# Gated delta net: decay times, their operands and a mask product moved from GpSimd to VectorE

## The chip, the cores and the metric

One core of one Trainium2 chip runs the whole program in one launch. The metric is device time in microseconds (us), the median of the runs of one kernel. A profile is one further execution, recorded instruction by instruction. The engines are named as in its rows: PE (TensorE matmul) and PEld (its weight loads), DVE (VectorE), ACT (ScalarE), POOL (GpSimd), SP (SyncE, which issues the DMAs).

## The reference

A decoder layer for 2048 tokens of width 1024: an RMS norm, one input projection, four head groups side by side (retention, gated delta net, S5, gated linear attention), a gate for each, and one output projection. The change touches the gated delta net: 4 heads of width 64, in chunks of 64 tokens.

```python
gcum = jnp.cumsum(gc, axis=-1)
decay = jnp.exp(jnp.where(tri, gcum[..., :, None] - gcum[..., None, :], -jnp.inf))
kb = kc * bc[..., None]
a_mat = jnp.where(strict, jnp.einsum('bhnid,bhnjd->bhnij', kb, kc) * decay, 0.0)
sol = lax.linalg.triangular_solve(jnp.eye(c, dtype=F32) + a_mat, rhs, left_side=True, lower=True)
attn = jnp.einsum('bhnid,bhnjd->bhnij', qc, kc) * decay
def step(state, inp):
    v_new = u_n - jnp.einsum('bhcd,bhde->bhce', w_n, state)
    o = jnp.einsum('bhcd,bhde->bhce', qg_n, state) + jnp.einsum('bhij,bhje->bhie', attn_n, v_new)
    state = state * gl_n[..., None, None] + jnp.einsum('bhcd,bhce->bhde', kg_n, v_new)
```

## The kernel before, in words

Tokens lie in 16 tiles of 128 (two chunks each). The delta net (`phase_dn`) goes over 8 pairs of tiles, called u = 0 to 7, in rounds that overlap: round s runs the convolution and the decays of pair s (`conv` with `dn_pre` inside), the scores and the inverse of pair s-1 (`dn_front`, `dn_sub`) and the recurrence of pair s-2 (`dn_back`). A round lasts some 45 us, and the whole stretch runs from about 600 to 975 us of the span.

What the steps of the prediction name:
- `dgx`: operands of the decays, g (fp16) spread over 64 columns times a mask, 128x512 for each tile. TensorE multiplies them by constant matrices (L1568), ScalarE takes the exponential into `dE` (L1569).
- `dmb`: decay times mask (strict and not strict side by side), 128x512 for each tile, and then times `dD` (beta over the key's squared norm). `dD` comes at the end of a string of small VectorE operations (`dkk`, `dry`, `drt`).
- `dLT` and `dST` (L1638 and L1643 in the code, shown as L153 in rows because a helper records them): scores from PSUM (ring `t`, L1627) times `dmb`. `dLT` is written to memory and read back transposed for the inverse: a string of 28 small VectorE operations on `dsV` and `dgm`. The transposes L1660 need the slot in ring `t` that the last `dST` frees.
- `VS`, L1813: the state's subtraction on VectorE, four in a round (two tiles, two chunks). TensorE waits for it at L1818.
- `cva`: the convolution's multiply-adds, 128x256; `ckq` and `cv` close them. `raw` (L1473, ScalarE) takes the convolution's input out of PSUM, `pa` (L309, L301) are the projections that fill TensorE between the steps.
- `fss`, `fry`, `frt`, `frr`, `fsq`: the norm and gating of a finished tile (`finish`).

The order on each engine is set when the program is built: a scheduler places instructions by priority and by its own estimates, buffers of a pool are reused in turn, and each engine then runs its list strictly in order. `dgx` has two buffers, so that a `dgx` may start when the L1568 of two `dgx` before has read its buffer, long before its own L1568 needs it.

Of the kernel before, what the change touches and what calls it, by code (L numbers as in the profile page):

```python
# [11 lines left out]
ALU = mybir.AluOpType  # L12
# [143 lines left out]
class Trunk:  # L156
# [1388 lines left out]
    def dn_pre(self, u, kq, out):  # L1545

        nc, NT = self.nc, self.NT
        P = self.dP  # L1550
        mask2 = self.c("mask2")
        tl = slice(2 * u, 2 * u + 2)
        gms = []
        for t in range(2):
            gm = self.t(P, [128, 256], "dgx", bufs=2).bitcast(F16).rearrange("p (g t) -> p g t", t=64)
            gms.append(gm)
            nc.gpsimd.tensor_tensor(gm, self.g16[:, 2 * u + t].rearrange("p a h -> p (a h)").unsqueeze(2).to_broadcast([128, 8, 64]), mask2[:, 64:128].unsqueeze(1).to_broadcast([128, 8, 64]), op=ALU.mult)
        yield
        E = self.t(P, [128, 2, 2, 4, 64], "dE", bufs=1)
        mb = self.t(P, [128, 2, 4, 2, 64], "dmb", bufs=1)  # L1560
        for t in range(2):
            gmf = gms[t].rearrange("p (a h) t -> p a (h t)", a=2)
            if t == 1:
                yield
            pe = self.ps("t")
            for j in range(2):
                for a in range(2):
                    nc.tensor.matmul(pe[:, j * 256:j * 256 + 256], self.sums16[:, j], gmf[:, a], start=(j == 0 and a == 0), stop=(j == 1 and a == 1))  # L1568
            nc.scalar.activation(E[:, t].rearrange("p a h t -> p (a h t)"), pe, AF.Exp)  # L1569
            nc.gpsimd.tensor_tensor(mb[:, t], E[:, t, 0].unsqueeze(2).to_broadcast([128, 4, 2, 64]),  # L1570
                                    mask2.rearrange("p (s t) -> p s t", s=2).unsqueeze(1).to_broadcast([128, 4, 2, 64]), op=ALU.mult)
        yield
        kq = kq[u]
        sq = self.t(P, [128, 2, 2, 256], "dsq", bufs=1)
        nc.scalar.activation(sq.rearrange("p s j t -> p (s j t)"), kq.rearrange("p s j t -> p (s j t)"), AF.Square)
        yield
        ps = self.ps("t")[:, 0:16]
        for t in range(2):
            for s in range(2):
                for j in range(2):  # L1580
                    o = t * 8 + s * 4 + j * 2
                    nc.tensor.matmul(ps[:, o:o + 2], sq[:, s, j, t * 128:t * 128 + 128], self.c("halves"), start=True, stop=True)  # L1582
        at = self.count["t"]

        ops = []
        V = Later(nc.vector, ops)
        p4 = ps.rearrange("p (t s h) -> p t s h", t=2, s=2)
        epsq = self.t(P, [128, 2, 4], "depsq", bufs=3)
        V.tensor_scalar(epsq, p4[:, :, 1], 4 * EPS, 16384 * EPS, op0=ALU.add, op1=ALU.mult)
        kk = self.t(P, [128, 8], "dkk")  # L1590
        k24 = kk.rearrange("p (t h) -> p t h", t=2)
        V.tensor_scalar(k24, p4[:, :, 0], 4 * EPS, None, op0=ALU.add)
        rk, more = self.rsqrt_ops(P, kk, None, 8, "dr")
        ops.extend(more)
        sk = self.t(P, [128, 8], "dsk")
        V.tensor_tensor(sk, kk, rk, op=ALU.mult)
        V.tensor_tensor(rk, rk, rk, op=ALU.mult)
        r24 = rk.rearrange("p (t h) -> p t h", t=2)
        D = self.t(P, [128, 2, 4], "dD")
        V.tensor_tensor(D, self.beta[:, tl, :], r24, op=ALU.mult)  # L1600
        kgd = self.t(P, [128, 2, 4], "dkgd", bufs=3)
        V.tensor_tensor(kgd, self.kgd[:, tl, :], r24, op=ALU.mult)
        gl = self.t(P, [128, 2, 4], "dgl", bufs=3)
        nc.gpsimd.tensor_copy(gl, E[:, :, 1, :, 63])
        for t in range(2):
            V.tensor_tensor(mb[:, t].rearrange("p h s i -> p h (s i)"), mb[:, t].rearrange("p h s i -> p h (s i)"),
                            D[:, t].unsqueeze(2).to_broadcast([128, 4, 128]), op=ALU.mult)
        out.update(gl=gl, epsq=epsq, kgd=kgd, sk=sk, E=E, mb=mb)
        self.string(18, 2, ops, "t", at)
        yield  # L1610
# [371 lines left out]
```

## Time and profile before

| what | value |
|---|---|
| median of 3 runs | 1224.54 us (1223.58 to 1227.66) |
| the profiled execution's own time | 1231.87 us |
| its span, first to last instruction | 1229.8 us |
| mean granted TensorE clock, as a share of full speed | 0.959 |
| PE busy in the span | 1116.9 us |
| DVE busy in the span | 911.0 us |
| POOL busy in the span | 471.1 us |

The profiled execution is 7.3 us over the median of the runs shown, and 2.1 us of its time lie outside the span. Times of instructions are read from the span, so differences worked out there are taken off the median.

### The profile page before, as it was taken

What the parts mean: (1) busy time and instruction counts of PE and PEld (TensorE: products, weight loads), DVE (VectorE), ACT (ScalarE), POOL (GpSimd) and SP (SyncE); (2) the same over time, 40 slices, a digit from 0 to 9 for tenths busy, and PEclk for the clock granted to TensorE, in tenths of its full rate; (3) what the DMA queues carried; (4) which work ended last, traced back from release to release, by engine and by line L of the source; (5) the groups of instructions that cost most, each with busy time, mean ns of one, the idle gap of its engine ahead of it and who ended that gap; (6) DMA issues with size and microseconds to landing.
All of it is one profiled execution on the core that took longest, in us unless ns stands there. A gap on an engine that the chain in (4) does not pass through costs nothing. (4 is left out here: it accounts for less than half of the span.)

```text
span 1229.8 us, 38305 instructions
## 1 busy us (share of the span) xinstructions
PE 1116.9 (91%) x15687; PEld 929.8 (76%) x15687; DVE 911.0 (74%) x3237; ACT 505.7 (41%) x1124; POOL 471.1 (38%) x848
## 2 busy tenths in 40 slices
PE   3889999999999999989779889898899999899996
PEld 2767788888878887877667677677777877788885
DVE  6779655445888788887797877877787744778885
ACT  5733322124444444453454344344443533443431
POOL 3112111111676666563552432533522312444433
PEclk9899999999989999999998998999899989999999
DMA  8565611201121111221212121211123616567652
GB/s 288 146 168 129 173 62 35 70 31 57 26 61 36 36 35 36 65 61 23 88 46 34 28 42 18 61 27 34 30 58 81 181 44 194 140 187 177 183 138 86
DMA packets 186911, 104.97 MB, mean 85 GB/s; under 512 B 158000, under 2 KB 173552, under 8 KB 184560
## 3 DMA queue, kind: packets, MB, share of 16 engines
q1 hardware_dynamic: 186160, 102.00, 32.1%
q8 instruction: 123, 2.02, 0.7%
q10 hardware_dynamic: 576, 0.52, 0.1%
q14 instruction: 52, 0.43, 0.1%
HBM read 59.43 MB, written 26.23 MB: 70 GB/s over the span
## 5 line engine op out<-in xcount | busy, mean ns | idle before, releaser
L301 PEld LDWEIGHTS <-xT 128*128 128x128 f16 x3456 | 337.4, 101 | 78.3 <-issue 22.0
L301 PE MATMUL pa<-w,xT 128*128 128x256 f16 x3072 | 384.4, 280 | 7.4 <-DVE w L265 3.3
L309 PE MATMUL pa<-xT,w 128*128 128x256 f16 x1536 | 202.4, 281 | 8.8 <-ACT raw L1473 7.0
L309 PEld LDWEIGHTS <-w 128*128 128x128 f16 x1536 | 147.7, 101 | 35.6 <-issue 11.1
L1858 PE MATMUL o<-w,yT 128*128 128x256 f16 x1344 | 155.5, 276 | 7.4 <-DMA yT<-y 7.3
L1858 PEld LDWEIGHTS <-yT 128*128 128x128 f16 x1344 | 132.5, 99 | 27.9 <-DMA yT<-y 10.0
L153 DVE SCALAR_TENSOR_TENSOR cva<-raw,cw,cva 128x256 f32<-128x256 f32 x144 | 80.3, 559 | 22.3 <-ACT cva L1478 20.8
L1869 POOL TENSOR_TENSOR ot<-of,npost 128x256 f32<-128x256 f32 x64 | 56.3, 898 | 50.7 <-ACT of L1867 50.7
L153 ACT ACTIVATE gE<-gE 128x384 f32<-128x384 f32 x96 | 45.6, 516 | 56.2 <-DVE gE L153 26.4
L153 DVE TENSOR_REDUCE fss<-fsq 128x4 f32<-128x256 f32 x48 | 19.8, 413 | 56.6 <-ACT fsq L408 56.6
L1472 POOL COPY raw<-raw 128x3 f32<-128x3 f32 x48 | 19.5, 413 | 110.1 <-DVE cva L153 75.1
L301 PE MATMUL pa<-wsu,xT 128*128 128x280 f16 x384 | 52.9, 298 | 7.4 <-DMA xT<-h 3.6
L265 DVE SCALAR_TENSOR_TENSOR w<-stg,wgs,w 128x256 f16<-128x256 f32 x96 | 50.3, 580 | 9.6 <-POOL w L262 9.6
L1147 POOL TENSOR_TENSOR ropq<-ropm,ropn 128x256 f32<-128x256 f32 x16 | 12.8, 797 | 113.4 <-DVE ropn L1144 105.4
L408 ACT ACTIVATE fsq<-o 128x256 f32<-128x256 f32 x48 | 18.2, 379 | 82.1 <-PE o L1195 57.5
L1868 DVE SCALAR_TENSOR_TENSOR ojk<-of 128x256 f32<-128x256 f32 x64 | 40.0, 625 | 14.2 <-ACT of L1867 11.7
L371 ACT ACTIVATE th<-pa,hd 128x256 f32<-128x256 f32 x64 | 30.1, 470 | 42.8 <-PE pa L301 40.4
L1484 ACT ACTIVATE cvt<-cva 128x256 f32<-128x256 f32 x48 | 20.0, 416 | 65.0 <-DVE cva L153 64.8
L1179 POOL TENSOR_TENSOR sg<-sbd,cst 64x128 f32<-64x128 f32 x30 | 12.8, 425 | 80.4 <-DVE sbd L1180 68.8
L1299 PE MATMUL sc<-gE 32*32 32x32 f32 (+1 forms) x2944 | 39.7, 200 | 1.5 <-DVE KK L910 1.5
L1299 PEld LDWEIGHTS sc<-gE 32*32 32x32 f32 (+1 forms) x2944 | 33.8, 105 | 8.8 <-issue 2.1
L1804 POOL TENSOR_TENSOR dKG<-dkh,dkgd 64x256 f32<-64x256 f32 x32 | 21.9, 683 | 47.2 <-PE c L1818 47.2
(420 smaller groups left out, 2329.1 us busy)
## 6 DMA issues: line engine op xcount, KB each, us to landing
x<-in_x SPq DMA_DIRECT2D x16, 512.0 KB, 4.4
stg<-in_wi SPq DMA_DIRECT2D x8, 1024.0 KB, 5.0
yo<-y_d SPq DMA_DIRECT2D x14, 512.0 KB, 4.4
xo<-in_x SPq DMA_DIRECT2D x14, 512.0 KB, 3.6
out<-xo SPq DMA_DIRECT2D x13, 512.0 KB, 3.8
y_d<-fsq SPq DMA_DIRECT2D x48, 128.0 KB, 1.8
xT<-in_wi SPq DMA_DIRECT2D x4, 1024.0 KB, 7.5
rope<-in_rope SPq DMA_DIRECT2D x16, 256.0 KB, 3.0
```

Of the source, the lines that this page charges most:

```text
L153: return lambda *a, **k: self.ops.append(lambda: getattr(self.engine, name)(*a, **k))
L265: nc.vector.scalar_tensor_tensor(dst[:, 1, k, :], st[:, k, :], gs[:, k:k + 1], dst[:, 0, k, :], op0=ALU.mult, op1=ALU.subtract)
L301: yield lambda k=k, i=i, a=a, b=b: self.nc.tensor.matmul(out, xt[:, a, k, t0:t0 + 128], w[:, b, k, :], start=(k == 0 and i == 0), stop=(k ...
L309: yield lambda k=k, i=i, a=a, b=b: self.nc.tensor.matmul(out, w[:, b, k, c0:c0 + 128], xt[:, a, k, :], start=(k == 0 and i == 0), stop=(k ...
L371: nc.scalar.activation(th, ps[0], AF.Tanh, scale=self.half(dsc))
L1299: nc.tensor.matmul(box[0][po:po + pn, e, c0:c0 + rh.shape[1]], lh[r], rh[r], start=True, stop=True, tile_position=(32 * (2 * hp + e), col))
L1472: nc.gpsimd.tensor_copy(x[:, 0:3], x[:, 256:259])
L1484: nc.scalar.activation(th[0], a, AF.Tanh, scale=0.5)
L1804: nc.gpsimd.tensor_tensor(KG[r, c], f["kh"][r, t], f["kgd"][r, t, :].unsqueeze(2).to_broadcast([64, 4, 64]), op=ALU.mult)
L1858: nc.tensor.matmul(o, yT[:, a, k, :], w[:, b, k, :], start=(k == 0 and q == 0 and j % per == 0), stop=(k == 7 and q == 2 and j % per == pe ...
L1868: nc.vector.scalar_tensor_tensor(jk, of[:, cs], 1.0, of[:, cs], op0=ALU.mult, op1=ALU.mult, accum_out=so[:, j:j + 1])
L1869: nc.gpsimd.tensor_tensor(t1[:, cs], of[:, cs], npost[:, cs], op=ALU.mult)
```

## The change

The two `dgx` of each pair are made on VectorE in place of GpSimd, with the same operands (L1557). GpSimd no longer multiplies decay by mask (L1570). VectorE makes decay times `dD` times mask in one `scalar_tensor_tensor` for each tile and head (128x128 each, eight for a pair), with `dD` as the scalar of each partition, in place of one `tensor_tensor` of 128x512 for each tile.

```diff
-            nc.gpsimd.tensor_tensor(gm, self.g16[:, 2 * u + t].rearrange("p a h -> p (a h)").unsqueeze(2).to_broadcast([128, 8, 64]), mask2[:, 64:128].unsqueeze(1).to_broadcast([128, 8, 64]), op=ALU.mult)
+            nc.vector.tensor_tensor(gm, self.g16[:, 2 * u + t].rearrange("p a h -> p (a h)").unsqueeze(2).to_broadcast([128, 8, 64]), mask2[:, 64:128].unsqueeze(1).to_broadcast([128, 8, 64]), op=ALU.mult)
...
-            nc.gpsimd.tensor_tensor(mb[:, t], E[:, t, 0].unsqueeze(2).to_broadcast([128, 4, 2, 64]),
-                                    mask2.rearrange("p (s t) -> p s t", s=2).unsqueeze(1).to_broadcast([128, 4, 2, 64]), op=ALU.mult)
...
+        m3 = mask2.rearrange("p (s t) -> p s t", s=2)
         for t in range(2):
-            V.tensor_tensor(mb[:, t].rearrange("p h s i -> p h (s i)"), mb[:, t].rearrange("p h s i -> p h (s i)"),
-                            D[:, t].unsqueeze(2).to_broadcast([128, 4, 128]), op=ALU.mult)
+            for h in range(4):
+                V.scalar_tensor_tensor(mb[:, t, h], E[:, t, 0, h].unsqueeze(1).to_broadcast([128, 2, 64]), D[:, t, h:h + 1], m3, op0=ALU.mult, op1=ALU.mult)
```

The scheduler also orders the stretch anew, on all engines but SP. Three places follow. The first is VectorE's list in the round of pair 6's convolution, around the third of the four `VS` of pair 4 (the second tile's first chunk). Before:

```order
L153 COPY dsV_14122<-dsV_14122 64x256
L153 TENSOR_TENSOR frt_14449<-fry_14448 128x4
L153 SCALAR_TENSOR_TENSOR frt_14449<-frt_14449,fss_14446 128x4
L153 SCALAR_TENSOR_TENSOR fry_14448<-frt_14449,fry_14448 128x4
L153 TENSOR_TENSOR frt_14449<-fry_14448 128x4
L153 SCALAR_TENSOR_TENSOR frt_14449<-frt_14449,fss_14446 128x4
L153 SCALAR_TENSOR_TENSOR frt_14449<-frt_14449 128x4
L153 SCALAR_TENSOR_TENSOR fry_14448<-frt_14449,fry_14448 128x4
L1813 TENSOR_TENSOR VS_14246<-dQ_14237,c_14437 64x256
L153 TENSOR_SCALAR frr_14447<-fry_14448,hd_1657_11455 128x4
```

In the changed kernel, at the same place:

```order
L153 TENSOR_TENSOR dgm_14150<-dsV_14146 64x15
L153 SCALAR_TENSOR_TENSOR fry_14471<-frt_14472,fry_14471 128x4
L153 TENSOR_TENSOR dsV_14146<-dsV_14146,dgm_14150 64x15
L153 TENSOR_TENSOR frt_14472<-fry_14471 128x4
L153 COPY dsV_14146<-dsV_14146 64x256
L153 SCALAR_TENSOR_TENSOR frt_14472<-frt_14472,fss_14469 128x4
L1812 TENSOR_TENSOR VS_14270<-dQ_14261,c_14460 64x256
L153 SCALAR_TENSOR_TENSOR frt_14472<-frt_14472 128x4
L153 SCALAR_TENSOR_TENSOR fry_14471<-frt_14472,fry_14471 128x4
L153 TENSOR_SCALAR frr_14470<-fry_14471,hd_1657_11462 128x4
```

The third `VS` stood behind all of the norm's string but its last scale (`frr`); now two more operations of that string come behind it. In the rounds of the convolutions of pairs 3, 4, 5 and 7 the third `VS` has moved ahead of four, four, eight and four small operations.

The second place is VectorE's list from `dD` to `dLT` of pair 6, where the next round begins. Before:

```order
L153 TENSOR_TENSOR dD_14590<-beta_3619,dry_14587 128x8
L153 TENSOR_TENSOR dkgd_14591<-kgd_4207,dry_14587 128x8
L153 SCALAR_TENSOR_TENSOR fsq_14818<-o_14537,frr_14602,dgg_14498 128x64
L153 TENSOR_TENSOR dmb_14398<-dmb_14398,dD_14590 128x512 x2
L153 SCALAR_TENSOR_TENSOR fsq_14818<-o_14537,frr_14602,dgg_14498 128x64 x3
L153 TENSOR_TENSOR dLT_14842<-t_14716,dmb_14398 128x4x64
L153 TENSOR_TENSOR dLT_14842<-t_14717,dmb_14398 128x4x64
```

In the changed kernel:

```order
L153 TENSOR_TENSOR dD_14612<-beta_3619,dry_14609 128x8
L153 TENSOR_TENSOR dkgd_14613<-kgd_4207,dry_14609 128x8
L153 SCALAR_TENSOR_TENSOR fsq_14846<-o_14559,frr_14624,dgg_14520 128x64
L153 SCALAR_TENSOR_TENSOR dmb_14422<-dE_14421,dD_14612,cst_75 128x128 x8
L153 SCALAR_TENSOR_TENSOR fsq_14846<-o_14559,frr_14624,dgg_14520 128x64 x2
L153 TENSOR_TENSOR dLT_14870<-t_14744,dmb_14422 128x4x64
L153 TENSOR_TENSOR dLT_14870<-t_14745,dmb_14422 128x4x64
```

The two `dmb` of 512 columns have become eight of 128 columns, at the same place: behind `dD`, ahead of `dLT`.

The third place is where the `dgx` of pair 7 are made, in the round of pair 6's convolution. Before, on GpSimd:

```order
L1805 TENSOR_TENSOR dKG_14411<-cst_75,dgl_13101 64x256
L1472 COPY raw_1507_10267<-raw_1507_10267 128x3
L1557 TENSOR_TENSOR dgx_15049<-g_709_4199,cst_75 128x512
L1570 TENSOR_TENSOR dmb_14398<-dE_14397,cst_75 128x512
L1688 MEMSET dsV_14879 64x256
L1690 MEMSET dsV_14879 64x16
L1557 TENSOR_TENSOR dgx_15051<-g_709_4199,cst_75 128x512
L1570 TENSOR_TENSOR dmb_14398<-dE_14397,cst_75 128x512
```

In the changed kernel it stands in VectorE's list, between the strings of the inverse and behind the second `VS`:

```order
L1488 SCALAR_TENSOR_TENSOR ckq_14135<-cvt_14353,cva_14310 128x256
L153 TENSOR_TENSOR dgm_14150<-dsV_14146 64x63
L1812 TENSOR_TENSOR VS_13701<-dQ_14261,c_14361 64x256
L153 TENSOR_TENSOR dsV_14146<-dsV_14146,dgm_14150 64x9x7
L1557 TENSOR_TENSOR dgx_15077<-g_709_4199,cst_75 128x512
L153 TENSOR_TENSOR dgm_14150<-dsV_14146 64x60
```

This first `dgx` of a pair waits there for TensorE (its buffer's last reader, L1568); the second stands behind the fourth `VS` and carries no wait. In the first round the two `dgx` of pair 0 stand directly behind the last two `w` (L265) of VectorE's list.

## Rows read from the trace of the kernel before

**Rows 1.** The page: span, and busy time of each engine.
```profile
span 1229.8 us, 38305 instructions
...
PE 1116.9 (91%) x15687; PEld 929.8 (76%) x15687; DVE 911.0 (74%) x3237; ACT 505.7 (41%) x1124; POOL 471.1 (38%) x848
```

**Rows 2.** Windows, delta net: stretch; PE, PEld, DVE, ACT, POOL busy; PEclk, DMA.
```profile
600.00:960.00 360.00, 318.71 (x4905) 255.11 (x4903) 291.35 (x957) 156.60 (x355) 143.97 (x232) 0.94 0.22 49
```

**Rows 3.** Groups on PE, 600 to 975 us: count, busy, mean ns, idle before, releasers.
```profile
L309 PE MATMUL pa<-xT,w 128*128 128x256 f16 x1096 | 146.4, 283 | 7.2 <-ACT raw L1473 7.0
L1818 PE MATMUL c<-VS,dKG 128*64 128x64 f32 x224 | 19.8, 234 | 15.0 <-DVE VS L1813 6.3 <-DVE frr L153 5.0 <-DVE fry L153 2.1
L1582 PE MATMUL t<-cst,dsq 128*128 128x2 f32 x128 | 17.1, 264 | 2.3 <-ACT dsq L1575 2.3
L1660 PE MATMUL t<-cst,ckq 128*128 128x128 f32 x32 | 5.4, 295 | 2.1 <-DVE dST L153 2.1
```

**Rows 4.** Groups on POOL, 600 to 975 us, the two that go.
```profile
L1570 POOL TENSOR_TENSOR dmb<-dE,cst 128x512 f32<-128x512 f32 x16 | 21.9, 1366 | 0.0
L1557 POOL TENSOR_TENSOR dgx<-g,cst 128x512 f16<-128x512 f16 x16 | 17.6, 1101 | 13.2 <-PE t L1568 13.2
```

**Rows 5.** Groups on DVE, 600 to 960 us.
```profile
L153 DVE SCALAR_TENSOR_TENSOR cva<-raw,cw,cva 128x256 f32<-128x256 f32 x144 | 80.3, 559 | 22.3 <-ACT cva L1478 20.8
L153 DVE TENSOR_TENSOR dmb<-dmb,dD 128x512 f32<-128x512 f32 x16 | 10.7, 684 | 0.0
```

**Rows 6.** The tile cva: shortest, median, longest ns; first and last start.
```profile
L153 DVE SCALAR_TENSOR_TENSOR cva<-raw,cw,cva x144: 467/478/2053, 601.1 to 934.1; 128x256 f32<-128x256 f32 x144
```

**Rows 7.** Timeline before the third VS, one round: start, us, instruction, [idle before].
```profile
865.48 1.17 DVE L153 TENSOR_TENSOR dsV<-dsV,dgm 64x39 f32<-64x39 f32 x1
865.56 1.03 POOL L1557 TENSOR_TENSOR dgx<-g,cst 128x512 f16<-128x512 f16 x1
...
866.56 1.27 POOL L1570 TENSOR_TENSOR dmb<-dE,cst 128x512 f32<-128x512 f32 x1
...
866.91 0.96 DVE L153 TENSOR_TENSOR dgm<-dsV 64x28 f32<-64x28 f32 x1
...
868.13 0.17 DVE L153 TENSOR_TENSOR dsV<-dsV,dgm 64x28 f32<-64x28 f32 x1
...
870.21 0.16 DVE L153 SCALAR_TENSOR_TENSOR fry<-frt,fry 128x4 f32<-128x4 f32 x1
870.40 0.41 DVE L1813 TENSOR_TENSOR VS<-dQ,c 64x256 f32<-64x256 f32 x1
...
870.96 0.65 PE L1818 MATMUL c<-VS,dKG 128*64 128x64 f32 x8 [2.48 <-DVE frr L153]
870.99 0.86 DVE L153 SCALAR_TENSOR_TENSOR fsq<-o,frr,dgg 128x64 f32<-128x64 f32 x4
```

**Rows 8.** Timelines of DVE, POOL and PE at the stretch's start.
```profile
603.03 0.87 DVE L265 SCALAR_TENSOR_TENSOR w<-stg,wgs,w 128x256 f16<-128x256 f32 x2
...
605.34 2.29 POOL L1557 TENSOR_TENSOR dgx<-g,cst 128x512 f16<-128x512 f16 x2
...
606.50 0.60 PE L1568 MATMUL t<-dgx,cst 128*128 128x256 f16 x4 [2.24 <-POOL dgx L1557]
```

**Rows 9.** Timeline from dmb to the transposes, pair 6.
```profile
895.18 1.28 DVE L153 TENSOR_TENSOR dmb<-dmb,dD 128x512 f32<-128x512 f32 x2
...
897.95 1.52 DVE L153 TENSOR_TENSOR dST<-t,dmb 64x256 f32<-64x256 f32 x4
...
899.65 0.66 PE L1660 MATMUL t<-cst,ckq 128*128 128x128 f32 x4
```

**Rows 10.** Windows around two waits before L1818, columns as in group 2.
```profile
776.80:780.20 3.40, 3.40 (x22) 2.44 (x23) 1.21 (x5) 1.62 (x4) 0.78 (x3) 0.50 0.32 70
865.00:872.40 7.40, 4.92 (x50) 4.02 (x48) 6.58 (x26) 1.48 (x4) 3.05 (x5) 1.00 0.17 18
872.40:879.20 6.80, 6.80 (x48) 4.87 (x47) 2.91 (x5) 1.77 (x5) 3.42 (x7) 0.50 0.54 100
```

## The prediction

> **What bounds the kernel now.** I read the page's totals first [rows 1]: TensorE is busy for 1116.9 of 1229.8 us, VectorE for 911.0, GpSimd for 471.1. No engine is full, so what counts is which wait ends last in the stretch that the change touches. The windows give that stretch [rows 2]: between 600 and 960 us TensorE is busy for 319 of 360 us, VectorE for 291, GpSimd for 144. TensorE is idle for 41 us in all, and that is about the most that shorter waits alone can give. The groups of TensorE's instructions say what it waits for [rows 3]: 15.0 us ahead of L1818, 13.4 of them (6.3 + 5.0 + 2.1) ended by VectorE, in seven waits, 1.9 us each; 7.0 us ahead of L309, for a `raw` on ScalarE that stands behind the convolution's steps; 2.3 and 2.1 us at L1582 and L1660. GpSimd, by name, ends one wait, the 2.2 us before the first decays [rows 8]. It costs more than that through VectorE, as the next view shows.
>
> **What GpSimd's 512-column operations cost VectorE.** The timeline before one L1818 [rows 7]: `dsV` 64x39 starts at 865.48 and takes 1.17 us, while GpSimd runs a `dgx` from 865.56 to 866.59; `dgm` 64x28 takes 0.96 us and ends at 867.87, while GpSimd runs a `dmb` that ends at 867.83. The next small operation of that kind, with nothing beside it, takes 0.17 us. So VectorE lost about 1.0 us to the one and 0.8 us to the other, and the subtraction `VS` at 870.40, for which TensorE stood idle for 2.48 us, came 1.8 us later for it. The same loss shows in the convolution's step: 559 ns in the mean against a median of 478, over 144 instructions [rows 5, 6], 11.7 us on that group alone.
>
> How much goes with the change: 32 GpSimd operations, 39.5 us of work [rows 4]. At 0.8 to 1.0 us each it would be up to 31 us. The lower bound: only the 11.7 us of the convolution's group, by these operations' share of GpSimd's busy time (39.5 of 144, 27% [rows 2, 4]), 3 us. I take 22 us, 0.7 us each: the two rows show nearly the full loss where VectorE has work on two tensors of SBUF at the time, and it is busy for 291 of 360 us, but some of them will fall on idle or on work from PSUM.
>
> **What VectorE gets instead.** Two instructions of one kind in a row cost less than twice their recorded duration, so I take rows of several. Two `dmb` of 512 columns take 1.28 us [rows 9], 0.64 each. Four scaled steps of 64 columns take 0.86 us [rows 7], 0.215 each; two of 256 columns take 0.87 us [rows 8], 0.435 each; a 128-column step lies between at 0.29 us. Removed: 16 x 0.64 = 10.2 us. Added: 64 x 0.29 = 18.6 us of scaled products and 16 `dgx` of 512 columns. No row shows this `dgx` on VectorE; I take the 0.64 us of the `dmb` row (bounds 0.4, if fp16 went faster, and GpSimd's own 1.1), 10.2 us, bounds 6 to 18. Together +18.6 us, bounds +14 to +26. The new instructions will meet GpSimd's other work too, which is 104 us of the 360 [rows 2, 4]: 0 to 5 us, I take 3. VectorE's sum is then 18.6 + 3 - 22, about zero. The change is no saving for VectorE; what matters is where time goes and where it comes.
>
> For the scaled products the Trainium skill speaks against the change: its Vector Engine (DVE) Microarchitecture Reference, "Points that are easy to get wrong", says that a scalar_tensor_tensor with two SBUF sources that are not bf16 runs at half throughput. By its clock of 0.96 GHz that would be, as an estimate from that page, some 0.13 us more for each of the 64, or 8.5 us. The convolution's steps are of this very kind (two fp32 tensors in SBUF, a scalar for each partition), and 256 columns in 478 ns [rows 6] leave no room for it, so the sum goes by the rows.
>
> **Place by place.** Terms are TensorE's idle time, minus being gain.
> - The third `VS`. Of the seven waits' 13.4 us [rows 3], the shown one loses 1.8 us of delay, gets one `dgx` of 0.64 ahead of it, and has two to eight small operations less in front (0.19 us each, from 870.21 to 870.40 [rows 7]): 1.5 to 2.7 us less, against a wait of 2.48. Not every round has both GpSimd operations just there. I take -8, bounds 0 and -13.4.
> - The first decays. The two `w` end at 603.90 [rows 8]; a `dgx` behind them is done by 604.6 in place of GpSimd's first at about 606.4. The wait is 2.24 us, I take -1.5 (bounds 0, -2.2), since the convolution's steps behind it come later by two `dgx`.
> - L309 behind `raw`: 7.0 us [rows 3], which hang on the convolution's steps. I take -2, bounds 0 and -5.
> - L1582, behind the second `dgx` and the last `ckq`: it loses the GpSimd pair, gets 0.64 us. I take -1.5 of 2.3 us, bounds 0 and -2.3.
> - From `dD` to the transposes: eight products take 2.3 us for 1.28, so `dLT` and `dST` come 1.0 us later. In pair 6 the last `dST` ends at 899.47 and L1660 starts at 899.65 [rows 9], so some 0.8 us of TensorE's time is at risk. With 1.0 us for pair 0, where it waits already [rows 3], and the same 0.8 for one more I get +2.6; elsewhere `dLT` has to wait for the scores or there is room. Bounds 0 and +8 (all eight).
> - The `dgx` in VectorE's list wait for TensorE. On GpSimd such waits were 13.2 us in all [rows 4] and held nothing up; in VectorE's list the convolution and the next `VS` are queued behind. The list places them later than GpSimd took them, so I take +2, bounds 0 and +13.
>
> Sum: -8 - 1.5 - 2 - 1.5 + 2.6 + 2 = -8.4 us. GpSimd's relief itself counts nothing, since its remaining work (`dST`, the copies for `raw`) waits for VectorE already. The profiled execution would go from 1231.87 to 1223.5 us, the median from 1224.54 to about 1216.
>
> **The rivals.** Less than 0.3% either way, 3.7 us, is about what a measurement of this kernel can't tell from no change.
> - *More, through the clock.* After the wait at 870 us TensorE, which had been busy for 4.92 of 7.40 us at full clock, was granted 0.50, the lower level of 1.2 GHz, for 6.8 us, and after another wait of this kind for 3.4 us, busy throughout [rows 10]. At 2.4 GHz this work would take half, 5.1 us less. If these waits go and others like them, -8.4 becomes -14 to -20: 1204 to 1211 us. Against it: other stretches at half clock follow other waits. Chance 0.14.
> - *Nothing.* What TensorE gets back at L1818 it loses at the next wait, since VectorE has no less to do in a round than before. The sum of VectorE's times speaks for it, and TensorE's idle time being spread over many waits. 1221 to 1228 us. Chance 0.22.
> - *Slower: VectorE stands at the first `dgx` of each pair.* For it: GpSimd waited 13.2 us there, and the third order excerpt has `dgx` right behind the second `VS`, in front of the string of the inverse. If VectorE loses all 13.2 us, the term of +2 becomes +13.2, and the third `VS` comes as late as before, so that the 8 us fall away: -8.4 + 11.2 + 8 = +10.8, 1235 us. Against it: the list gives VectorE two small operations and a `VS` to do meanwhile. It decides from about 1.3 us for each of the eight on, where 2 + 8.4 us are used up. Chance 0.20.
>
> **How the numbers follow.** The forecast, 1211 to 1221 us with 1216 as its point, has a chance of 0.44; its own bounds are wider, but the terms with large bounds (the third `VS`, the wait at `dgx`) are the rivals. For 8 in 10 the range goes from 1205, most of the clock's case, to 1231, where a part of the slower case is left out. Faster by over 0.3%: 0.44 + 0.14, and 0.58 with nothing from the case of no change. Within 0.3%: 0.21. Slower: 0.21.
>
> **What would show it.** In the profile after: the mean of the convolution's step near 510 ns, and the idle time before L1818 at 5 to 8 us for 15.0; scaled products of 128 columns at about 0.29 us from start to start (0.34 recorded) and `dgx` at 0.64; VectorE's busy time in the stretch about the same, GpSimd's down by 39 us; small gains in TensorE's idle time at L1568 and L1582, a small loss at L1660. The step on contention is wrong if the convolution's mean stays near 560. The prediction is wrong if `dgx` on VectorE shows idle time of several us before it, ended by L1568, if the `dST` make L1660 wait in most rounds, or if TensorE's idle time only moves to other lines.

## The result, and the profile after

The changed kernel takes 1211.71 us in the median of 5 runs (1205.45 to 1214.07), the kernel before 1224.54 (1223.4 to 1227.66, 5 runs): a ratio of 0.988, 95% interval 0.984 to 0.992, or 12.8 us less. Two further comparisons in the experiments below give 0.990 [0.987, 0.993] each, 13.3 and 11.7 us. Forecast were 1216 us, 8.5 us less, in a range of 1205 to 1231. Of all executions in this document one, of the kernel with two steps below, lies more than 1.5% over the fastest of its kernel, and it is left out.

The profiled executions lie 26.2 us apart in span, twice that, since the one of before was 7.3 us over its median and the one of after, at 1205.45 us, 6.3 us under. The page after, with the busy times:

```profile
span 1203.6 us, 38349 instructions
...
PE 1106.2 (92%) x15687; PEld 924.5 (77%) x15687; DVE 901.4 (75%) x3301; ACT 505.4 (42%) x1124; POOL 434.6 (36%) x816
```

VectorE makes 64 instructions more than before [rows 1] and is busy for 9.6 us less; GpSimd loses 36.5 us. A window of a fixed length catches more of the program in the faster kernel, so I compare the stretch between two events: from the first convolution step (the first `cva` on ScalarE) to the start of the last `VS`. The windows of that stretch, first for the kernel before:

```profile
598.80:1015.70 416.90, 373.03 (x5667) 298.41 (x5665) 323.73 (x1072) 183.49 (x414) 156.81 (x252) 0.94 0.24 56
```

And for the changed kernel:

```profile
598.10:994.80 396.70, 367.37 (x5666) 295.98 (x5665) 314.44 (x1135) 182.82 (x414) 120.14 (x220) 0.96 0.26 59
```

The columns are those of [rows 2]. Of the 20.2 us that the stretch is shorter, 14.6 are TensorE's idle time (the length less PE's busy time: 43.9 before, 29.3 after); 5.6 are busy time of about the same matmuls, at a mean granted clock of 0.96 for 0.94 (the column before the last two). VectorE is busy for 9.3 us less though it does more.

TensorE's groups between 600 and 975 us, the answer to [rows 3]:

```profile
L309 PE MATMUL pa<-xT,w 128*128 128x256 f16 x1090 | 145.8, 283 | 3.2 <-ACT raw L1473 2.8 <-DVE wv L253 0.2
...
L1817 PE MATMUL c<-VS,dKG 128*64 128x64 f32 x224 | 18.9, 227 | 5.1 <-DVE dgm L153 1.8 <-DVE frt L153 1.0 <-DVE dsV L153 0.9
...
L1580 PE MATMUL t<-cst,dsq 128*128 128x2 f32 x128 | 15.5, 252 | 4.5 <-ACT dsq L1573 4.5
...
L1568 PE MATMUL t<-dgx,cst 128*128 128x256 f16 x64 | 10.3, 283 | 0.6 <-ACT dE L1569 0.4 <-DVE dgx L1557 0.3
...
L1659 PE MATMUL t<-cst,ckq 128*128 128x128 f32 x32 | 4.9, 275 | 0.2 <-DVE dST L153 0.2
```

VectorE's groups there, the answer to [rows 5], with the new work:

```profile
L153 DVE SCALAR_TENSOR_TENSOR cva<-raw,cw,cva 128x256 f32<-128x256 f32 x144 | 69.8, 491 | 17.2 <-ACT cva L1478 16.0
...
L153 DVE SCALAR_TENSOR_TENSOR dmb<-dE,dD,cst 128x128 f32<-128x128 f32 x64 | 19.2, 365 | 0.0
...
L1557 DVE TENSOR_TENSOR dgx<-g,cst 128x512 f16<-128x512 f16 x16 | 11.0, 686 | 0.9 <-PE t L1568 0.7
```

The convolution's steps went from 559 to 491 ns in the mean (median 478 before, 479 after; the longest took 2053 ns and now takes 829, so what went is the length of the long ones), and the 144 steps alone give back 10.5 us. The wait at L1818 (now L1817) fell from 15.0 to 5.1 us. VectorE waits 0.7 us in all for L1568's buffers.

At the place of [rows 7], the third `VS` of pair 4 (VectorE's timeline, then TensorE's):

```profile
855.41 0.17 DVE L153 TENSOR_TENSOR dsV<-dsV,dgm 64x15 f32<-64x15 f32 x1
855.50 0.14 DVE L153 TENSOR_TENSOR frt<-fry 128x4 f32<-128x4 f32 x1
855.62 0.37 DVE L153 COPY dsV<-dsV 64x256 f32<-64x256 f32 x1
855.91 0.15 DVE L153 SCALAR_TENSOR_TENSOR frt<-frt,fss 128x4 f32<-128x4 f32 x1
856.09 0.41 DVE L1812 TENSOR_TENSOR VS<-dQ,c 64x256 f32<-64x256 f32 x1
...
856.65 0.53 PE L1817 MATMUL c<-VS,dKG 128*64 128x64 f32 x6 [0.47 <-DVE frt L153]
```

The wait is 0.47 us where it was 2.48: VectorE runs its small operations here at 0.14 to 0.17 us, none of them stretched to 1 us. From 851 to 854 us, beside `dKG` on GpSimd, four operations of the same string still take 0.31 to 0.62 us where their like take about 0.2.

From `dD` to the `dST` of pair 6, the answer to [rows 9]:

```profile
878.23 2.18 DVE L153 SCALAR_TENSOR_TENSOR dmb<-dE,dD,cst 128x128 f32<-128x128 f32 x8
...
881.70 1.52 DVE L153 TENSOR_TENSOR dST<-t,dmb 64x256 f32<-64x256 f32 x4
```

Eight products take 2.18 us, 0.27 each from start to start (0.29 taken in the forecast).

### The profile page after: what moved, and what is told of

It is laid out like the page before. It is cut to its first block, busy times and chain, and to the rows that moved or that the text cites. A ratio compares the mean times of both kernels' runs of the same rounds, so it can differ in the third digit from the quotient of the medians.

```text
span 1203.6 us, 38349 instructions
## 1 busy us (share of the span) xinstructions
PE 1106.2 (92%) x15687; PEld 924.5 (77%) x15687; DVE 901.4 (75%) x3301; ACT 505.4 (42%) x1124; POOL 434.6 (36%) x816
## 5 line engine op out<-in xcount | busy, mean ns | idle before, releaser
L301 PEld LDWEIGHTS <-xT 128*128 128x128 f16 x3456 | 336.4, 100 | 76.2 <-issue 21.5
L301 PE MATMUL pa<-w,xT 128*128 128x256 f16 x3072 | 380.1, 278 | 6.4 <-DVE w L265 3.1
L309 PE MATMUL pa<-xT,w 128*128 128x256 f16 x1536 | 203.0, 282 | 4.7 <-ACT raw L1473 2.8
L309 PEld LDWEIGHTS <-w 128*128 128x128 f16 x1536 | 147.4, 101 | 32.3 <-issue 7.5
L1857 PE MATMUL o<-w,yT 128*128 128x256 f16 x1344 | 152.3, 273 | 7.3 <-DMA yT<-y 7.3
L1857 PEld LDWEIGHTS <-yT 128*128 128x128 f16 x1344 | 130.7, 98 | 26.3 <-DMA yT<-y 10.1
L153 DVE SCALAR_TENSOR_TENSOR cva<-raw,cw,cva 128x256 f32<-128x256 f32 x144 | 69.8, 491 | 17.2 <-ACT cva L1478 16.0
L265 DVE SCALAR_TENSOR_TENSOR w<-stg,wgs,w 128x256 f16<-128x256 f32 x96 | 49.3, 569 | 8.9 <-POOL w L262 8.9
L1867 DVE SCALAR_TENSOR_TENSOR ojk<-of 128x256 f32<-128x256 f32 x64 | 40.3, 630 | 10.1 <-ACT of L1866 7.6
L1179 POOL TENSOR_TENSOR sg<-sbd,cst 64x128 f32<-64x128 f32 x30 | 12.8, 425 | 82.7 <-DVE sbd L1180 70.7
L1803 POOL TENSOR_TENSOR dKG<-dkh,dkgd 64x256 f32<-64x256 f32 x32 | 22.2, 693 | 47.9 <-PE c L1817 47.5
```

What stands on the lines that cost most here:

```text
L153: return lambda *a, **k: self.ops.append(lambda: getattr(self.engine, name)(*a, **k))
L265: nc.vector.scalar_tensor_tensor(dst[:, 1, k, :], st[:, k, :], gs[:, k:k + 1], dst[:, 0, k, :], op0=ALU.mult, op1=ALU.subtract)
L301: yield lambda k=k, i=i, a=a, b=b: self.nc.tensor.matmul(out, xt[:, a, k, t0:t0 + 128], w[:, b, k, :], start=(k == 0 and i == 0), stop=(k ...
L309: yield lambda k=k, i=i, a=a, b=b: self.nc.tensor.matmul(out, w[:, b, k, c0:c0 + 128], xt[:, a, k, :], start=(k == 0 and i == 0), stop=(k ...
L1803: nc.gpsimd.tensor_tensor(KG[r, c], f["kh"][r, t], f["kgd"][r, t, :].unsqueeze(2).to_broadcast([64, 4, 64]), op=ALU.mult)
L1857: nc.tensor.matmul(o, yT[:, a, k, :], w[:, b, k, :], start=(k == 0 and q == 0 and j % per == 0), stop=(k == 7 and q == 2 and j % per == pe ...
```

## The experiments

The theory: GpSimd's two operations of 512 columns, while they read SBUF, held up VectorE's instructions that read two tensors there; the gain is what VectorE gets back. Rivals: the gain comes from the new order of the lists (the third `VS`, the first decays); it comes from GpSimd's queue being shorter; it comes from the granted clock. The kernels were timed in three groups of four, each together with the kernel before; its median is 1224.91 us in the first group (the changed kernel again, idle products, fills, `dgx` alone), 1229.2 in the second (the products alone, two steps, the first `dKG` product, copies) and 1224.38 in the third. Ratios are to it. The second group does not have the changed kernel in it, and the one kernel that was in the second group and in the third came out at 0.984 and 0.990: between groups, differences up to some 0.6% tell nothing. The texts on the half clock mean TensorE's busy time inside stretches that were granted 0.50, halved.

**The changed kernel again.** No edit.

> The changed kernel once more, timed in the same rounds as the next three so that they can be set against it; every theory expects the time measured for it, 1212 us, 12 to 13 us under the kernel before. A second profile tells what part of the first one's 26 us over before is the execution: the profiled run of before lay 7 us over its median, that of after 6 us under its own. Contention theory (GpSimd's two 512-column operations held VectorE up): VectorE's convolution steps again near 490 ns in the mean for 559 before, and TensorE's idle time from the start of the convolutions to the last VS near 29 us for 44 before. Clock theory (the gain is mostly TensorE's granted clock): the time at half clock in that stretch is again some 17 us less than before; if it differs from the first profile by more than the gain, the clock is the execution's and not the change's.

1211.65 us, ratio 0.990 [0.987, 0.993]. In its profile the stretch reads:

```profile
594.10:996.40 402.30, 372.65 (x5667) 299.37 (x5665) 314.45 (x1136) 182.94 (x414) 120.64 (x220) 0.94 0.25 58
```

TensorE's idle time is 29.7 us (29.3 in the first profile), VectorE's busy time 314.45 (314.44); the convolution's steps take 491 ns. TensorE's busy time is 5.3 us more at a lower granted clock. So in this kernel waits and VectorE's time repeat from execution to execution, and TensorE's busy time doesn't. In one other kernel the waits did not repeat: with the first `dKG` product moved too, further down, TensorE's idle time is 26.4 us in one profile and 34.8 in the next.

**GpSimd makes its products all the same, for nobody.** The scratch tile is small, so each product is made in two halves.

```diff
+            dms = self.t(P, [128, 128], "dms", bufs=1).bitcast(F16).rearrange("p (h t) -> p h t", t=64)
+            for a in range(2):
+                nc.gpsimd.tensor_tensor(dms, self.g16[:, 2 * u + t, a].unsqueeze(2).to_broadcast([128, 4, 64]), mask2[:, 64:128].unsqueeze(1).to_broadcast([128, 4, 64]), op=ALU.mult)
...
             nc.scalar.activation(E[:, t].rearrange("p a h t -> p (a h t)"), pe, AF.Exp)
+            for s in range(2):
+                nc.gpsimd.tensor_tensor(dms, E[:, t, 0], mask2[:, s * 64:s * 64 + 64].unsqueeze(1).to_broadcast([128, 4, 64]), op=ALU.mult)
```

> The changed kernel, and GpSimd in addition makes the two products that it made before (spread g times mask, decay times mask), at the places where it made them, into a small tile of fp16 that nobody reads. All other engines' lists are word for word those of the changed kernel. Contention theory: VectorE's convolution steps go back from 491 to about 550 ns, VectorE loses some 20 us in the stretch, TensorE waits longer before L1817, and the time is 6 to 13 us over the changed kernel: 1218 to 1225 us. Order theory (the gain comes from the third VS and the decays standing earlier in the lists, whatever GpSimd does): within 2 us of the changed kernel, 1210 to 1214 us. If the result lies between, the difference to the changed kernel is contention's part and the rest, to before, is the order's.

1234.94 us (1228.11 to 1237.47), ratio 1.0087 [1.006, 1.011]: 23.3 us over the changed kernel, where the contention theory had given 6 to 13 and the order theory at most 2, and 10.0 over the kernel before. The lists of TensorE, VectorE and ScalarE are those of the changed kernel, row for row. VectorE and GpSimd in the round of pair 6's convolution, where the last `dgx` is made:

```profile
874.71 1.26 DVE L1557 TENSOR_TENSOR dgx<-g,cst 128x512 f16<-128x512 f16 x1
875.89 2.10 DVE L153 SCALAR_TENSOR_TENSOR cva<-raw,cw,cva 128x256 f32<-128x256 f32 x3
...
874.70 0.72 POOL L1574 TENSOR_TENSOR dms<-dE,cst 128x256 f16<-128x256 f32 x1
875.37 0.66 POOL L1607 COPY dgl<-dE 128x8 f32<-128x8 f32 x1
875.99 0.97 POOL L1574 TENSOR_TENSOR dms<-dE,cst 128x256 f16<-128x256 f32 x1
877.03 2.34 POOL L1560 TENSOR_TENSOR dms<-g,cst 128x256 f16<-128x256 f16 x3
```

The same two rows of VectorE in the changed kernel, with GpSimd beside them only a short copy:

```profile
859.49 0.71 DVE L1557 TENSOR_TENSOR dgx<-g,cst 128x512 f16<-128x512 f16 x1
860.12 1.51 DVE L153 SCALAR_TENSOR_TENSOR cva<-raw,cw,cva 128x256 f32<-128x256 f32 x3
...
859.46 0.19 POOL L1602 COPY dgl<-dE 128x8 f32<-128x8 f32 x1
```

No wait is written beside VectorE's rows in the one or the other; the instructions are just longer, 1.26 for 0.71 us and 2.10 for 1.51. The wait before TensorE's L1817 (L1822 here) rises from 5.1 to 10.1 us:

```profile
L1822 PE MATMUL c<-VS,dKG 128*64 128x64 f32 x224 | 19.4, 230 | 10.1 <-DVE dsV L153 3.4 <-DVE frt L153 3.2 <-DVE dgm L153 2.7
```

Not all of the 23.3 us is that. GpSimd's list is longer too, and twice VectorE waits at L265 for a `w` that GpSimd makes behind the products:

```profile
789.61 1.09 DVE L265 SCALAR_TENSOR_TENSOR w<-stg,wgs,w 128x256 f16<-128x256 f32 x2 [3.16 <-POOL w L262]
...
885.41 1.09 DVE L265 SCALAR_TENSOR_TENSOR w<-stg,wgs,w 128x256 f16<-128x256 f32 x2 [3.18 <-POOL w L262]
```

The first of them in the changed kernel:

```profile
776.75 1.09 DVE L265 SCALAR_TENSOR_TENSOR w<-stg,wgs,w 128x256 f16<-128x256 f32 x2 [0.69 <-POOL w L262]
```

In the whole stretch VectorE waits 9.1 us for this `w` with idle products, 4.1 in each of the three profiles of the changed kernel, and 4.8 and 5.4 in the two of before: GpSimd's queue has a part of up to 5.0 us in this run, and about 1 us in the change itself, where the forecast had put GpSimd's relief at nothing. The clock has a part as well. The mean granted clock is 0.953 over the six executions with idle products, 0.961 over the 17 of the changed kernel and 0.963 over the 58 of the kernel before. Between executions of one kernel, 0.01 of it goes with some 9 us (the common slope of lines through the executions of each kernel), so by this estimate 7 of the 23.3 us and 8 of the 10.0 go with the lower clock. At one clock, then, by the same estimate, putting the products back costs some 16 us: it takes back the gain and little more. Why the clock is lower there is not shown. The halves take GpSimd 54.0 us for the 39.5 of [rows 4], but they hold VectorE up about as much (the table further down: 21.5 us, 23.7 before).

**GpSimd fills the tile instead.**

```diff
+            for _ in range(6):
+                nc.gpsimd.memset(dms, 0.0)
```

stands at both places, in place of the idle products.

> As the run with the idle products, but GpSimd fills the small tile with zeros at these places, six times for each product, about as long as a product took by the fills' own rows (306 ns for 64x256); a fill reads nothing from SBUF. The other lists are again those of the changed kernel. Contention theory, in the form that it is the reading of two tensors by GpSimd that holds VectorE: the time of the changed kernel within 2 us, 1210 to 1214, and convolution steps near 490 ns. Rival: it is GpSimd's queue, its other operations (dST, dKG, the copies for raw) coming later by what stands ahead of them, that costs: then 1216 to 1224 us, as with idle products, with VectorE's convolution steps at 490 ns.

1210.41 us, ratio 0.990 [0.986, 0.994]: that of the changed kernel. One thing was not as the text says: the fills wait for nothing, and GpSimd ran all 192 of them (205 ns each, 39.4 us) between 603 and 670 us, in the first rounds, not spread over all. There they are a strong test: between 600 and 670 us GpSimd is busy for 59.3 of 70 us, with idle products for 42.9, and yet VectorE is busy for 52.1 us here, with 174 instructions (0.30 us each), and for 58.3 us there, with 169 (0.35 each). In the changed kernel it is 56.7 us with 186 (0.30 each).

```profile
600.00:670.00 70.00, 62.03 (x646) 52.12 (x644) 52.06 (x174) 31.55 (x65) 59.30 (x238) 0.85 0.26 65
```

So a busy GpSimd costs nothing here by itself; its reading does. The rival of GpSimd's queue is refuted for these rounds. In the later ones the fills no longer stand in the queue; what the queue costs there is seen in the waits at L265 above.

**GpSimd copies instead.** Two copies of 128x256 in place of each product:

```diff
+            for _ in range(2):
+                nc.gpsimd.tensor_copy(dms, E[:, t, 0])
```

> As the run with idle products, but GpSimd copies in place of multiplying: two copies of 128x256 for each product, of the decay or of the mask spread over four heads, into the small fp16 tile, so that it reads one tensor of SBUF and not two. All other lists are those of the changed kernel. If VectorE is held by any GpSimd operation that reads SBUF: VectorE loses 10 to 20 us in the stretch, by the length of the copies, and the time is 1220 to 1232 us. If it needs two tensors read by GpSimd: as with the memsets, 1208 to 1214 us.

1218.77 us, ratio 0.993 [0.990, 0.996]: between the changed kernel and before, about 4 us over the changed kernel by the ratios (0.990 to 0.993) and 6 to 7 by the times, but the two were not in one group, so that the traces say more than the total here. At the place shown above, `dgx` takes 0.92 us beside a copy of 0.39:

```profile
870.49 0.92 DVE L1557 TENSOR_TENSOR dgx<-g,cst 128x512 f16<-128x512 f16 x1
871.34 1.54 DVE L153 SCALAR_TENSOR_TENSOR cva<-raw,cw,cva 128x256 f32<-128x256 f32 x3
...
870.48 0.39 POOL L1574 CAST dms<-dE 128x256 f16<-128x256 f32 x1
```

Neither expectation was met: reading one tensor holds VectorE too, but by less, 5.4 us for 37.4 us of copies where products cost 21.5 for 54.0.

**Each part of the change alone.** `dgx` alone moves L1557's `nc.gpsimd` to `nc.vector` and leaves the rest as before; the products alone are the changed kernel with L1557 back on `nc.gpsimd`.

> Of the change only the first part: the two dgx of each pair on VectorE, the product of decay and mask on GpSimd and the multiplication by dD in 512 columns on VectorE as before. The build gives it an order of its own. Contention theory: in the trace of before, of VectorE's 52.6 us over the shortest durations 8.8 fall to the dgx and 14.9 to the product, so dgx alone brings about a third of the gain, less VectorE's 11 us for the dgx themselves: 3 to 5 us, 1219 to 1222 us. Order theory: the decays and the third VS come earlier with the dgx, so that this part alone brings most of the gain: 1211 to 1215 us.

1222.42 us, ratio 0.998 [0.996, 1.001]: 2.5 us less, not clear of no change. The order theory had given it most of the gain, and that failed; the contention theory had given 3 to 5. TensorE's idle time in the stretch is 37.2 us, 6.9 under that of before (44.1, the mean of two profiles), at a mean granted clock of 0.960 for 0.963.

```profile
L1557 DVE TENSOR_TENSOR dgx<-g,cst 128x512 f16<-128x512 f16 x16 | 14.6, 915 | 3.9 <-PE t L1568 3.6
```

With GpSimd still multiplying decay by mask, VectorE's `dgx` take 915 ns in place of 686 and wait 3.6 us for L1568.

> Of the change only the second part: decay times dD times mask by eight operations of 128 columns on VectorE, no product on GpSimd; the dgx stay on GpSimd. The build gives it an order of its own. Contention theory, sized by what the run with idle products and the changed kernel show (21 us of VectorE's time and 24 us of the total for both parts, two thirds of them by the product of decay and mask): VectorE gets back 15 us, gives 8.4 us more for the scaled products, and the time is 1214 to 1219 us, nearer to the changed kernel than the other part alone was (1222). Order theory: the two parts need each other, since only together they let the third VS move up, so that this part alone gives no more than the other alone, 1220 to 1225 us.

1216.32 us where before took 1229.2 (the contention theory: 1214 to 1219), ratio 0.9896 [0.986, 0.993]. By the ratio that is the whole gain; by the time it is some 4 us over the changed kernel, which was not in this group. The trace is clearer: TensorE's idle time is 36.1 us, 8.0 under that of before. The two parts alone, 6.9 and 8.0 us, add up to what both save together, 14.9 (44.1 less 29.2, the mean of three profiles). So both parts count, and the totals of the parts alone are not exact enough to share the gain out.

**GpSimd relieved, but without the fused form.**

```diff
-            nc.gpsimd.tensor_tensor(mb[:, t], E[:, t, 0].unsqueeze(2).to_broadcast([128, 4, 2, 64]),
+            nc.vector.tensor_tensor(mb[:, t], E[:, t, 0].unsqueeze(2).to_broadcast([128, 4, 2, 64]),
```

in the kernel before, with `dgx` on VectorE too.

> The dgx on VectorE as in the changed kernel; the product of decay and mask also on VectorE, but by one operation of 512 columns for each tile straight behind the exponential, and the multiplication by dD in 512 columns as before. GpSimd has as little to do as in the changed kernel. Contention theory: it is GpSimd's relief that pays, not the fused form: VectorE spends 4 x 0.64 = 2.6 us a pair here, 2.3 to 2.4 in the changed kernel; from dD to dLT it is 1.0 us a pair shorter. So within 3 us of the changed kernel, 1209 to 1215 us. Rival, that the fused form itself brings the gain, by the place of the work behind dD, where VectorE has time: 1216 to 1222 us, since 1.3 us a pair then stand among the convolution's steps.

1214.94 us in the median of five, ratio 0.990 [0.985, 0.995], that of the changed kernel as far as different groups can be compared; TensorE's idle time is 31.8 us. Its products cost VectorE 10.9 + 10.5 us in 32 instructions, the fused ones 19.2 in 64. Who does the product decides; that the way it is written matters is not seen.

**More of GpSimd's reads moved.** In the changed kernel, `dKG`'s identity times decay (L1804) goes to VectorE, and in the second kernel the key times its scale (L1803) as well.

```diff
-                nc.gpsimd.tensor_tensor(KG[r, c], f["kh"][r, t], f["kgd"][r, t, :].unsqueeze(2).to_broadcast([64, 4, 64]), op=ALU.mult)
-                nc.gpsimd.tensor_tensor(KG[ro, c], id64[ro].unsqueeze(1).to_broadcast([64, 4, 64]), f["gl"][ro, t, :].unsqueeze(2).to_broadcast([64, 4, 64]), op=ALU.mult)
+                nc.vector.tensor_tensor(KG[r, c], f["kh"][r, t], f["kgd"][r, t, :].unsqueeze(2).to_broadcast([64, 4, 64]), op=ALU.mult)
+                nc.vector.tensor_tensor(KG[ro, c], id64[ro].unsqueeze(1).to_broadcast([64, 4, 64]), f["gl"][ro, t, :].unsqueeze(2).to_broadcast([64, 4, 64]), op=ALU.mult)
```

> The changed kernel, and one more of GpSimd's products moved to VectorE: identity times the chunk's decay into dKG (64x256, 32 of them), which GpSimd makes in 0.66 us each and by which VectorE loses 10.0 us in the changed kernel's stretch. VectorE pays some 0.36 us each, by the 402 to 420 ns of VS, which has the same shape and one operand in PSUM: 11 to 13 us. Contention theory: about even for VectorE, so 1208 to 1215 us; faster only if the dKG of a tile, which GpSimd makes before L1817 may start, were late, and no row shows L1817 waiting for it by more than 0.7 us. Rival: any relief of GpSimd pays as the first did, 1203 to 1208 us.

> The changed kernel again, in the same rounds as the version with the chunk's decay on VectorE, since those two were timed in different calls (1.0 and 1.6 per cent under before). Expected by every theory: 1.0 to 1.2 per cent under the kernel before. In the profile, TensorE's idle time from the first convolution step to the last VS within 1 us of the 29.3 and 29.5 us of the two earlier profiles, while what the half clock costs there (16.8 and 21.8 us) goes its own way.

> The chunk's decay times identity on VectorE, beside the changed kernel in the same rounds. If the first result stands: 5 to 8 us under the changed kernel. If it was the difference of two calls: within 3 us of it. By VectorE's own sum it should be even or slower: 30 operations at 0.42 us, 12.6 us, against 6 us of hold-ups that went; what speaks for a gain is that TensorE waits 1.0 us before L1817 in place of 5.1.

> Both products of dKG on VectorE, the key times its scale too (64x256, 32 of them, by which VectorE loses 10.5 us when GpSimd makes them). VectorE pays 32 x 0.42 = 13.4 us for 10.5, and it makes them between the steps of the recurrence itself, where GpSimd did it beside. By VectorE's sum: 2 to 6 us slower than with the first product alone. If any relief of GpSimd pays, as the first two did: 3 to 8 us faster than with the first alone, under 1200 us.

The first product alone came out at 1207.76 us where before took 1229.2 (0.984 [0.980, 0.987]), and at 1212.28 us in the third group (0.990 [0.987, 0.994]), where the changed kernel took 1212.67 (0.990 [0.987, 0.993]): the first result did not come again, and beside the changed kernel there is no difference. Both products together took 1206.49 us (1202.85 to 1215.71), 0.986 [0.982, 0.990], against the expectation by VectorE's sum, and without the rival's time under 1200 us: 6.2 us under the changed kernel in the median, but the intervals overlap, so that it stays likely and not shown. In its one profile the stretch has the least idle time of TensorE (25.5 us) and the least busy time of VectorE of all kernels:

```profile
597.00:996.40 399.40, 373.91 (x5666) 297.95 (x5665) 312.45 (x1199) 183.36 (x414) 85.99 (x156) 0.94 0.26 58
```

**The kernel before again.**

> The kernel before once more, for a second profile. Idle theory: TensorE's idle time from the first convolution step to the last VS, 43.9 us in the first profile, comes again within 2 us, so that the change's idle gain is 14 to 15 us, and the time that half clock costs there (25.2 us) is nearer to the changed kernel's 17 to 22: the gain of the medians is idle time. Clock theory: the half clock costs 25 us again, and part of the gain is the clock's. By the rounds the time is that of before within 0.3 per cent.

1224.23 us, ratio 0.999 [0.997, 1.002]. TensorE's idle time in the stretch is 44.3 us, 43.9 in the first profile:

```profile
595.80:1015.70 419.90, 375.56 (x5667) 300.13 (x5666) 321.07 (x1072) 183.45 (x414) 156.72 (x252) 0.93 0.25 56
```

All runs side by side. VectorE's busy time and TensorE's idle time are those of the stretch, from rows like the ones above. The hold-up is worked out from the trace between 600 and 960 us: for each form of VectorE instruction the time that one in ten stays under, and what each instruction took beyond it, from 40 ns on; each is put down to the GpSimd instruction that lies beside it longest, and the second figure is the share put down to the work that the change or the run is about. In the first profile of the kernel before, 123 instructions took such extra time, and every one has a GpSimd instruction beside it; of the other 833, 616 have none.

| kernel | ratio | DVE busy, us | PE idle, us | hold-up, us |
|---|---|---|---|---|
| idle products | 1.009 | 336.9 | 42.2 | 55.0, of it 21.5 the products |
| before (two profiles) | 1 | 323.7, 321.1 | 43.9, 44.3 | 52.6, 49.9, of it 23.7, 23.6 |
| dgx alone | 0.998 | 322.3 | 37.2 | 45.8, of it 16.7 the product |
| idle copies | 0.993 | 321.0 | 30.5 | 39.6, of it 5.4 the copies |
| first dKG product too (two) | 0.984, 0.990 | 320.1, 319.7 | 26.4, 34.8 | 27.8, 27.0 |
| products alone | 0.990 | 317.4 | 36.1 | 41.2, of it 10.5 the dgx |
| two steps on VectorE | 0.990 | 315.9 | 31.8 | 31.0 |
| changed (three) | 0.988, 0.990, 0.990 | 314.4, 314.5, 314.7 | 29.3, 29.7, 28.6 | 34.0, 33.8, 33.4 |
| idle fills | 0.990 | 314.0 | 29.2 | 33.4, of it 0.3 the fills |
| both dKG products too | 0.986 | 312.5 | 25.5 | 10.3 |

## Why the prediction was right, point by point

**The step on contention** was right, and is shown: with the order kept row for row and only GpSimd's products put back, VectorE's instructions are as long as before (21.5 us of hold-up by the products), and 23.3 us come back, of which the lower clock and GpSimd's queue have the parts said above. The forecast had VectorE get back 22 us and lose 3 to the new work's own meetings with GpSimd. The hold-up fell from 52.6 to 34.0 us (49.9 in the second profile of before): the 23.7 that fell to the two operations went, and some 5 came back, most of it at the `dKG`: 16 to 19 in all, where 19 were forecast.

The Trainium skill, page "SBUF — State Buffer", section "Who interferes with whom", under "The single rule", says that VectorE and GpSimd share a pair of ports, and that a VectorE instruction with two SBUF inputs contends with a GpSimd instruction that reads SBUF, but not with one that only writes it. On GpSimd's side the runs agree: products 21.5 us, copies 5.4, fills 0.3. No run here shows the ports themselves.

**The step on VectorE's sum** was a little off. The new work was sized well: 0.27 us for a scaled product (0.29), 0.60 for a `dgx`, which starts at 603.11 with the next instruction at 603.71 (0.64). Steps of 256 columns, of the same kind as the products, follow each other here at 0.41 us:

```profile
604.65 2.46 DVE L153 SCALAR_TENSOR_TENSOR cva<-raw,cw,cva 128x256 f32<-128x256 f32 x6
```

The rule that the forecast weighed, from the Trainium skill's Vector Engine (DVE) Microarchitecture Reference, section "Points that are easy to get wrong", would have made each product dearer by 0.13 us. The products alone, at 0.27 us for 128 columns, could not tell; the steps can: at half throughput, by that page's clock, 256 columns would take 0.53 us as an estimate, and they take 0.41. But VectorE's busy time did not stay level, it fell by 9.3 us (6.6 against the second profile). I counted what instructions lose to GpSimd; VectorE's busy time also counts how far neighbours in its list overlap, and that changed with the order. What part of the fall is due to that was not taken apart.

**Place by place**, idle times of TensorE in the first profiles:

| term | forecast | measured |
|---|---|---|
| third `VS`, L1818 | -8 | -9.9 (15.0 to 5.1) |
| first decays, L1568 | -1.5 | -1.6 (2.2 to 0.6) |
| L309 behind `raw` | -2 | -4.0 (7.2 to 3.2) |
| L1582 | -1.5 | +2.2 (2.3 to 4.5) |
| L1660, eight products for two | +2.6 | -1.9 (2.1 to 0.2) |
| VectorE at the `dgx` | +2 | 0.7 us of VectorE's waits |
| idle time of the stretch | -8.4 | -14.6 (43.9 to 29.3) |

In the second profile of before the five waits are 15.0, 2.2, 8.2, 1.3 and 0.6 us, so that the terms of L1582 and L1660 hold to 1 or 2 us only. One reading of the forecast was short: about all of the 15.0 us at L1818 were ended by VectorE, in nine waits, and not 13.4 in seven; the row names only the three largest causes.

The largest term and the sign held. The mis-sized ones are the two losses, +4.6 in the forecast and -1.9 in the traces, and they make up about all of what the forecast fell short by: the products do reach `dST` later (in pair 6, 5.18 us from the end of `dD` to the last `dST`, 4.58 before), but in the new order TensorE has other matmuls there, and waits 0.2 us at L1659 in the whole stretch; and the list places the `dgx` where L1568 has mostly run. The L1582 term has the wrong sign; that it was offset by larger gains at L1818 and L309 is luck. TensorE's waits in the first round, between 609 and 618 us, in the kernel before:

```profile
613.72 1.47 PE L309 MATMUL pa<-xT,w 128*128 128x256 f16 x12 [2.59 <-ACT raw L1473]
615.35 1.83 PE L1582 MATMUL t<-cst,dsq 128*128 128x2 f32 x15 [0.15 <-ACT dsq L1575]
```

And in the changed one:

```profile
609.30 4.53 PE L309 MATMUL pa<-xT,w 128*128 128x256 f16 x40 [1.02 <-ACT raw L1473]
...
616.47 0.72 PE L1580 MATMUL t<-cst,dsq 128*128 128x2 f32 x5 [2.64 <-ACT dsq L1573]
```

In this round the gain of the one line is about the loss of the other: 2.59 us at L309 become 1.02, and 0.15 at L1582 become 2.64 at L1580. Four `dgx` (two pairs') stand in VectorE's list between 603.11 and 608.56; that they delay `dsq` is likely and was not tried.

**The rivals.** *Nothing* is out by the intervals. *VectorE stands at the `dgx`*: 0.7 us for the 13.2 us feared; it did show where the product stayed on GpSimd (3.6 us). *More, through the clock*: the time lies close to that case's upper end, 1211 us, but not for its reason: the granted clock did not rise, it is 0.961 in the mean of the changed kernel's executions and 0.963 in that of the kernel before. TensorE's busy time in the stretch is 373.0 and 375.6 us before and 367.4, 372.7 and 377.2 after, so the same kernel differs by 10 us from one execution to the next, and the means (374.3 and 372.4) by 1.9; the idle times differ by 14.9 us between the kernels and by 1.1 within one. The gain of the medians, 12 to 13 us, is less than 14.9; at 9 us for 0.01 of the clock, the 0.002 that the changed kernel lies lower are worth some 2 us, an estimate that closes the gap.

Did the forecast miss in the whole how much of VectorE's time sets the end, though TensorE is busy for 93% of the stretch and VectorE for 79%? The table leans that way, but does not show it. From idle products to the changed kernel 22.5 us less of VectorE's busy time (336.9 to 314.4) come with 23.3 us less of the program, but a part of these is the clock's and the queue's; and the copies and the first `dKG` product, at 320 to 321 us, are level with the second profile of before (321.1) and yet have ratios of 0.984 to 0.993. TensorE's idle time is no full measure either: with idle products it is 42.2 us, less than before, at a time 10.0 us longer.

## What to carry to other kernels

An operation on a slack GpSimd is not free if it reads SBUF beside a VectorE whose results TensorE waits for: look at the spread of one form's durations on VectorE (median 478 ns, mean 559, longest 2053 [rows 5, 6]) and at what GpSimd does beside the long ones, since no wait shows. Do not share out a gain of 1% by the totals of its parts: here the parts alone came out at ratios of 0.998 and 0.990, as if one were worth nothing and the other all, while each of them saved about half of TensorE's idle time. To test such a reason, put the load back as work that nobody reads: the other lists stay as they are, so that the order is ruled out. Then read in its trace what else came with the load, here a longer queue on GpSimd and a lower clock, before the difference is put down to one cause.

## What the runs showed of the hardware that was not expected

Between 600 and 960 us, GpSimd's copies of one tensor hold VectorE up by about a third of what products of two tensors do: 5.4 us in 37.4 us of copies (14%), 21.5 in 54.0 us of products (40%), 0.3 in 39.4 us of fills. The hold is mutual where they meet: `dgl`, a copy of 128x8, takes GpSimd 0.19 us in the changed kernel and 0.66 when it starts in the middle of VectorE's `dgx` (875.37 in the run with idle products).

Not only VectorE's instructions with two tensors in SBUF are held. Two that read one tensor, in the whole kernel before:

```profile
L153 DVE TENSOR_REDUCE fss<-fsq x48: 400/414/421, 82.5 to 1018.5; 128x4 f32<-128x256 f32 x48
L153 DVE TENSOR_SCALAR fry<-fss x48: 151/170/653, 84.2 to 1019.1; 128x4 int32<-128x4 int32 x48
```

The sum `fss` keeps its length, though between 600 and 960 us 11 of its 12 lie beside GpSimd instructions that read; the shift that starts `fry` reaches 653 ns at a median of 170.
